# A hybrid recurrent layer: causal scores written by masked copies of VectorE and by ScalarE, gate product on VectorE

## The chip, the cores and the metric

The kernel runs on one core of a Trainium2 chip. A core has five engines that run side by side, each with its own list of instructions: PE (TensorE, matrix products, with PEld loading its weights), DVE (VectorE), ACT (ScalarE), POOL (GpSimd) and SP (SyncE, which here starts the DMA transfers). They meet only at semaphores. PE writes its results into PSUM, which DVE and ACT read; all other tiles lie in SBUF. The metric is the device time of one execution in microseconds (us): the median of three executions before the change is 2206.64 us (2205.87 to 2207.19).

## The reference, cut to what matters

One decoder layer on 2048 tokens of width 1024: an RMS norm, one input projection whose columns feed two token mixers, an output projection with residual, a SwiGLU feed-forward, a last norm. The change touches both mixers. The first (HGRN2, 4 heads of width 128) works on groups of 32 tokens:

```python
causal = jnp.tril(jnp.ones((CHUNK, CHUNK), dtype=bool))          # CHUNK = 32
def step(state, xs):
    q_, k_, lg, v_ = xs
    b = jnp.cumsum(lg, axis=-2)
    q_dec, k_dec = q_ * jnp.exp(b), k_ * jnp.exp(-b)
    scores = jnp.where(causal, jnp.einsum('bhtk,bhsk->bhts', q_dec, k_dec), 0.0)
    o = jnp.einsum('bhts,bhsv->bhtv', scores, v_) + jnp.einsum('bhtk,bhkv->bhtv', q_dec, state)
    ...
```

The second (RG-LRU, width 512 in 4 units of 128) computes `b_in = sqrt(-expm1(2 log_a)) * (ig * xc)` and a linear recurrence over the tokens. The product `ig * xc` is the other part that the change touches.

## The kernel before

The tokens are worked in two halves of 1024; each half has two chunks c of 512 tokens, and a chunk is four tiles of 128. A half runs a projection pv (the values), eight steps s, a gate projection pg, the output projection with residual, and the feed-forward. Full float precision is got by splitting each operand into a high and a low part, so a projection of one chunk is 24 matmuls of 128x512 (three per block of 128 inputs, L225 to L227).

A step projects two times 128 features, for chunk 0 and then chunk 1, into the PSUM banks pa and pb. Even steps (0, 2, 4, 6) are the four HGRN heads: `hg_pre` (sigmoids, logarithm, the scan L250 and some twenty small products) runs on ACT and DVE, and `hg_mid` and `hg_post` are put off into the projections of the step behind it. Odd steps are the four RG-LRU units (`lru_pre`, `lru_post`). Names carry their place: pb_3_0 is pb of step 3, chunk 0; sct_77 and sct_79 are the two score tiles that chunks 0 and 1 use in turn.

In `hg_mid` PE transposes the decayed keys into the bank pk (L320), DVE copies them to kut (L322), PE computes the scores of a chunk into the bank pc by 16 small matmuls (L329). The kernel works on tiles of 128 tokens, not of 32, and a score tile is stored transposed: rows are the source tokens, columns the target tokens, and only columns from a row's own block of 32 on are written by PE. Four DVE copies (L341) take these into the tile sct, each 32 columns of all four token tiles. Then POOL's affine_select (L342) sets to zero what lies below the diagonal. PE makes the state updates pu (L347), and DVE adds them up (L352, S and the carry). In `hg_post` PE computes the output po from the states (L364) and from the scores (L365), in turn for four tiles; ACT squares it (L370), POOL takes the inverse root, DVE scales it into v (L373). In `lru_post` POOL does the product ig * xc (L414); DVE and ACT do the rest.

The order on every engine isn't written out: the program is traced in the order of the code, and a scheduler with its own estimate of durations then puts each engine's instructions in order and adds the semaphores. Instructions of two engines that use the same PSUM bank are kept in order among each other. So an edit to a few lines can move instructions all over the input-projection stage.

Of the kernel before, what the change touches and what calls it, by code (L numbers as in the profile page):

```python
# [8 lines left out]
F32 = mybir.dt.float32  # L9
F32R = mybir.dt.float32r  # L10
AF = mybir.ActivationFunctionType
ALU = mybir.AluOpType

P = 128
# [9 lines left out]
CW = 512  # L24
NC = T // CW
TPC = CW // P
NTT = T // P
SUB = 32
# [7 lines left out]
def hybrid_layer(ctx: ExitStack, tc: tile.TileContext, x, x_t, norm_w, cols, w_in, gate_w, w_out, w_gu, w_down, out):  # L36
    nc = tc.nc
    const = ctx.enter_context(tc.tile_pool(name="const", bufs=1))
    sb = ctx.enter_context(tc.tile_pool(name="sb", bufs=1))
# [23 lines left out]
    def late(nm):  # L63
        return sb.tile([P, CW], F32, tag="late", name=nm, bufs=5)
# [4 lines left out]
    def aux(nm):  # L69
        return psp.tile([P, CW], F32, tag="aux", name=nm)  # L70
# [4 lines left out]
    mask = const.tile([P, CW], mybir.dt.bfloat16, name="mask")  # L75
    nc.gpsimd.memset(mask, 1.0)
    nc.gpsimd.memset(mask.rearrange("p (n s) -> p n s", s=SUB)[:, :, 0:1], 0.0)
    sc_t = []
    for i in range(2):
        s = const.tile([P, TPC, P], F32, name=f"sct{i}")  # L80
# [8 lines left out]
    v = nc.vector  # L89
# [225 lines left out]
    def hg_mid(h, c, st, vt, nm):  # L315
        hs = slice(h * P, (h + 1) * P)
        W, Wy, K, KU, G = (st[k] for k in ("W", "Wy", "K", "KU", "G"))
        pk = aux("pk" + nm)
        for n in range(TPC):
            nc.tensor.transpose(out=pk[:, n * P : (n + 1) * P], in_=KU[:, n * P : (n + 1) * P], identity=ident)  # L320
        kut = late("kut" + nm)
        v.tensor_copy(out=kut, in_=pk)  # L322

        pc = aux("pc" + nm)
        for n in range(TPC):
            o = n * P
            for j in range(4):
                r0 = j * SUB
                nc.tensor.matmul(  # L329
                    pc[r0 : r0 + SUB, o + r0 : o + P],  # L330
                    lhsT=K[:, o + r0 : o + r0 + SUB],
                    rhs=(W if j < 2 else Wy)[:, o + r0 : o + P],
                    start=True,
                    stop=True,
                )
        sc = sc_t[flip[0] % 2]
        flip[0] += 1
        pc4 = pc.rearrange("p (n t) -> p n t", t=P)
        for j in range(4):
            rows, cs = slice(0, (j + 1) * SUB), slice(j * SUB, (j + 1) * SUB)  # L340
            v.tensor_copy(out=sc[rows, :, cs], in_=pc4[rows, :, cs])  # L341
        nc.gpsimd.affine_select(  # L342
            out=sc, in_=sc, pattern=[[0, TPC], [1, P]], compare_op=ALU.is_ge, fill=0.0, base=0, channel_multiplier=-1
        )
        pu = aux("pu" + nm)
        for n in range(TPC):
            nc.tensor.matmul(pu[:, n * P : (n + 1) * P], lhsT=kut[:, n * P : (n + 1) * P], rhs=vt[:, n, hs], start=True, stop=True)  # L347

        S = late("S" + nm)
        states = [carry[:, c % 2, h, :]] + [S[:, n * P : (n + 1) * P] for n in range(TPC - 1)] + [carry[:, 1 - c % 2, h, :]]  # L350
        for n in range(TPC):
            v.scalar_tensor_tensor(  # L352
                out=states[n + 1], in0=states[n], scalar=G[:, n, 3:4], in1=pu[:, n * P : (n + 1) * P], op0=ALU.mult, op1=ALU.add
            )
        st["S"], st["sc"] = states, sc
# [44 lines left out]
    def lru_post(u, gl, xc, xh, xl, y, nm):  # L400
        pr, pi = aux("pr" + nm), aux("pi" + nm)
        for m, pg in enumerate((pr, pi)):
            gs = slice((m * NU + u) * P, (m * NU + u + 1) * P)
            nc.tensor.matmul(pg, lhsT=gwh[:, gs], rhs=xh, start=True, stop=False)
            nc.tensor.matmul(pg, lhsT=gwl[:, gs], rhs=xh, start=False, stop=False)
            nc.tensor.matmul(pg, lhsT=gwh[:, gs], rhs=xl, start=False, stop=True)
        r, ig, t = late("r" + nm), late("ig" + nm), late("t" + nm)
        us = slice(u, u + 1)
        nc.scalar.activation(out=r, in_=pr, func=AF.Sigmoid, bias=par[:, C_BA + u : C_BA + u + 1])
        nc.scalar.activation(out=ig, in_=pi, func=AF.Sigmoid, bias=par[:, C_BX + u : C_BX + u + 1])  # L410

        nc.scalar.activation(out=t, in_=r, func=AF.Tanh, scale=msp[:, us])
        nc.scalar.activation(out=r, in_=r, func=AF.Exp, scale=nmsp[:, us])
        nc.gpsimd.tensor_tensor(out=ig, in0=ig, in1=xc, op=ALU.mult)  # L414
        v.tensor_tensor(out=xc, in0=r, in1=r, op=ALU.mult)
        v.scalar_tensor_tensor(out=t, in0=xc, scalar=1.0, in1=t, op0=ALU.add, op1=ALU.mult)
        nc.scalar.activation(out=t, in_=t, func=AF.Sqrt)
        v.tensor_tensor(out=ig, in0=ig, in1=t, op=ALU.mult)
        v.tensor_tensor_scan(out=t, data0=r, data1=ig, initial=hst[:, us], op0=ALU.mult, op1=ALU.add)
        nc.gpsimd.tensor_copy(out=hst[:, us], in_=t[:, CW - 1 : CW])  # L420
        v.tensor_tensor(out=y[:, u, :], in0=t, in1=gl, op=ALU.mult)
# [454 lines left out]
    for half in range(2):  # L876
# [36 lines left out]
        for s in range(8):  # L913
            i = s // 2
            ws.ahead(2)
            wa, wb = ws.take(2)
            ws.ahead(2)
            for c in range(NC):
                nm = f"{half}_{s}_{c}"
                pa = feat_mm(wa, xt[c], "pa" + nm)  # L920
                run_pending()
                pb = feat_mm(wb, xt[c], "pb" + nm)
                if s % 2 == 0:
                    st = hg_pre(i, pa, pb, nm)
                    nxt = [
                        lambda i=i, st=st, c=c, nm=nm: hg_mid(i, c, st, vts[c], nm),
                        lambda i=i, st=st, c=c, nm=nm: hg_post(i, st, vts[c], nm),
                    ]
                else:
                    r = lru_pre(i, pa, pb, nm)  # L930
                    nxt = [lambda i=i, r=r, c=c, nm=nm: lru_post(i, *r, ys[c], nm)]
                pend.append(nxt)
# [175 lines left out]
```

## Time and profile before

| | before |
|---|---|
| median of three executions | 2206.64 us |
| the profiled execution, its span | 2208.05 us, 2206.3 us |
| mean granted clock of TensorE | 0.985 of full speed |
| busy: PE | 2121.9 us, 96% |
| busy: DVE, ACT, POOL | 1508.5, 1019.4, 587.7 us |

The span runs from the first to the last instruction of the profiled execution. PE is busy nearly throughout; the view of waits names what it waited for, and for how long, and the timeline lists instructions with their start, duration and, in brackets, the idle time of their engine before them with what ended it. The granted clock is the share of full speed (2.4 GHz) at which PE was allowed to run. The steps of the first half lie between about 75 and 360 us, those of the second between about 500 and 800 us.

### The profile page before, as it was taken

The numbers are of one execution on the slowest core, as the hardware profiler recorded it, in microseconds if no ns is written. First come the engines' busy times: TensorE is split into PE (matmuls) and PEld (weight loads), VectorE is DVE, ScalarE is ACT, GpSimd is POOL, SyncE is SP. The second block draws the span as 40 slices with busy tenths as digits, with TensorE's granted clock in tenths as the row PEclk, the third lists the DMA queues.
The fourth block names the chain that finished last, engine by engine and source line by source line (L and its number), as shares of the span: only waits on it lengthen the run. The fifth ranks groups of instructions, "written<-read, shape, count | busy, mean of one in ns | idle before, by whom it ended". The sixth has DMA issues, their size and how long they took to land. (4 is left out here: it accounts for less than half of the span.)

```text
span 2206.3 us, 27183 instructions
## 1 busy us (share of the span) xinstructions
PE 2121.9 (96%) x9956; PEld 1744.7 (79%) x9956; DVE 1508.5 (68%) x2314; ACT 1019.4 (46%) x1757; POOL 587.7 (27%) x442
## 2 busy tenths in 40 slices
PE   8999899999999999999999998998999999998998
PEld 6778788887777887788888876887788888876876
DVE  5566664635677557866676579777767666679897
ACT  5467664535677545433333343444333333343443
POOL 1111110101111101223232146411323232356455
PEclk9999999999999999999999999999999999999999
DMA  6111105851110056423232264355423232355423
GB/s 220 58 39 39 39 20 169 285 167 30 38 39 29 20 181 230 150 98 106 91 125 91 96 227 164 115 160 169 134 91 124 91 124 91 105 209 196 153 86 139
DMA packets 137414, 261.33 MB, mean 118 GB/s; under 512 B 11072, under 2 KB 27456, under 8 KB 137280
## 3 DMA queue, kind: packets, MB, share of 16 engines
q1 hardware_dynamic: 137280, 259.59, 35.1%
q8 instruction: 78, 1.28, 0.2%
q14 instruction: 56, 0.46, 0.1%
HBM read 196.37 MB, written 63.18 MB: 118 GB/s over the span
## 5 line engine op out<-in xcount | busy, mean ns | idle before, releaser
L484 POOL TENSOR_TENSOR e<-u,e 128x512 f32<-128x512 f32 x44 | 77.3, 1757 | 525.3 <-ACT wgu_c L198 307.0
L484 POOL TENSOR_TENSOR hd<-hd,e 128x512 f32<-128x512 f32 x80 | 121.5, 1550 | 142.4 <-DVE e L484 142.3
L582 PE MATMUL quad_e<-act_e,wgu_e 128*128 128x512 f32 x528 | 129.2, 393 | 2.0 <-ACT wgu_e L198 1.9
L582 PE MATMUL quad_f<-act_f,wgu_f 128*128 128x512 f32 x528 | 127.1, 389 | 1.5 <-ACT wgu_f L198 1.5
L582 PE MATMUL quad_g<-act_d,wgu_d 128*128 128x512 f32 x528 | 127.6, 390 | 0.0
L582 PE MATMUL quad_a<-act_a,wgu_a 128*128 128x512 f32 x528 | 127.3, 389 | 0.0
L582 PE MATMUL quad_g<-act_g,wgu_g 128*128 128x512 f32 x528 | 127.1, 389 | 0.0
L582 PE MATMUL quad_a<-act_b,wgu_b 128*128 128x512 f32 x528 | 127.0, 389 | 0.0
L582 PE MATMUL quad_e<-act_c,wgu_c 128*128 128x512 f32 x528 | 126.8, 389 | 0.0
L582 PEld LDWEIGHTS quad_e<-act_e,wgu_e 128*128 128x128 f32 x528 | 100.1, 190 | 24.0 <-ACT wgu_e L198 2.6
L582 PEld LDWEIGHTS quad_f<-act_f,wgu_f 128*128 128x128 f32 x528 | 99.1, 188 | 22.4 <-ACT wgu_f L198 1.8
L582 PEld LDWEIGHTS quad_a<-act_a,wgu_a 128*128 128x128 f32 x528 | 98.9, 188 | 20.9 <-issue 0.4
L582 PEld LDWEIGHTS quad_a<-act_b,wgu_b 128*128 128x128 f32 x528 | 99.1, 188 | 20.6
L582 PEld LDWEIGHTS quad_e<-act_c,wgu_c 128*128 128x128 f32 x528 | 99.1, 188 | 20.6
L582 PEld LDWEIGHTS quad_g<-act_g,wgu_g 128*128 128x128 f32 x528 | 99.0, 188 | 20.6
L582 PEld LDWEIGHTS quad_g<-act_d,wgu_d 128*128 128x128 f32 x528 | 98.9, 188 | 20.4
L484 DVE TENSOR_TENSOR u<-u,quad_g 128x512 f32<-128x512 f32 x88 | 60.4, 686 | 79.3 <-PE quad_g L582 79.2
L226 PE MATMUL pb<-xn,wlo_in 128*128 128x512 f32 x256 | 102.7, 401 | 0.0
L225 PE MATMUL pb<-xn,whi_in 128*128 128x512 f32 x256 | 102.4, 400 | 0.0
L227 PE MATMUL pb<-xn,whi_in 128*128 128x512 f32 x256 | 101.8, 398 | 0.0
L155 DVE TENSOR_TENSOR wlo_in<-raw_in,whi_in 128x1024 fp32r<-128x1024 f32 x48 | 60.7, 1265 | 60.0 <-PE pv L238 40.6
L226 PE MATMUL pa<-xn,wlo_in 128*128 128x512 f32 x256 | 100.9, 394 | 0.0
(316 smaller groups left out, 5521.2 us busy)
## 6 DMA issues: line engine op xcount, KB each, us to landing
raw<-in_w_gu SPq DMA_DIRECT2D x88, 512.0 KB, 3.8
raw_in<-in_w_in SPq DMA_DIRECT2D x48, 512.0 KB, 3.5
ao_p<-as SPq DMA_DIRECT2D x76, 256.0 KB, 2.3
raw_o<-in_w_out SPq DMA_DIRECT2D x32, 512.0 KB, 4.7
x<-in_x SPq DMA_DIRECT2D x32, 256.0 KB, 5.3
xrh<-in_x SPq DMA_DIRECT2D x32, 256.0 KB, 3.9
h<-h SPq DMA_DIRECT2D x32, 256.0 KB, 3.7
hn<-hths SPq DMA_DIRECT2D x32, 256.0 KB, 4.5
```

Source lines behind the costliest of these rows:

```text
L155: v.tensor_tensor(out=lo, in0=raw, in1=f(hi), op=ALU.subtract)
L225: nc.tensor.matmul(ps, lhsT=whi[:, ks], rhs=hi, start=(k == 0), stop=False)
L226: nc.tensor.matmul(ps, lhsT=wlo[:, ks], rhs=hi, start=False, stop=False)
L227: nc.tensor.matmul(ps, lhsT=whi[:, ks], rhs=lo, start=False, stop=(k == KT - 1))
L484: (e or v).tensor_tensor(out=out, in0=a, in1=b, op=op)
L582: nc.tensor.matmul(ps, lhsT=w[:, s, ks], rhs=x, start=first and k + n == 0, stop=k == 3 and n == 2, skip_group_check=not first)
```

## The change

A constant `keep` is built once: a causal 32x32 mask of bytes, repeated in each of the four groups of 32 partitions. The four copies and the affine_select are replaced: for each group j of 32 rows, DVE copies the 32x32 diagonal block of each of the four token tiles from pc to sct where the mask is set (copy_predicated), and ACT copies the columns to the right of it (96, 64 and 32 columns per tile; none for j = 3). What lies below the diagonal is not written any more; sct is set to zero at the start, as before. In `lru_post` the product ig * xc moves from POOL to DVE.

```diff
--- before.py
+++ after.py
@@ -75,6 +75,15 @@
     mask = const.tile([P, CW], mybir.dt.bfloat16, name="mask")
     nc.gpsimd.memset(mask, 1.0)
     nc.gpsimd.memset(mask.rearrange("p (n s) -> p n s", s=SUB)[:, :, 0:1], 0.0)
+
+    keep = const.tile([P, SUB], mybir.dt.uint8, name="keep")
+    tri = sb.tile([P, CW], F32, tag="pg", name="tri", bufs=16)
+    nc.gpsimd.memset(tri, 1.0)
+    nc.gpsimd.affine_select(
+        out=tri[:, 0:P], in_=tri[:, 0:P], pattern=[[1, P]], compare_op=ALU.is_ge, fill=0.0, base=0, channel_multiplier=-1
+    )
+    for j in range(4):
+        nc.gpsimd.tensor_copy(out=keep[j * SUB : (j + 1) * SUB], in_=tri[j * SUB : (j + 1) * SUB, j * SUB : (j + 1) * SUB])
     sc_t = []
     for i in range(2):
         s = const.tile([P, TPC, P], F32, name=f"sct{i}")
@@ -337,11 +346,10 @@
         flip[0] += 1
         pc4 = pc.rearrange("p (n t) -> p n t", t=P)
         for j in range(4):
-            rows, cs = slice(0, (j + 1) * SUB), slice(j * SUB, (j + 1) * SUB)
-            v.tensor_copy(out=sc[rows, :, cs], in_=pc4[rows, :, cs])
-        nc.gpsimd.affine_select(
-            out=sc, in_=sc, pattern=[[0, TPC], [1, P]], compare_op=ALU.is_ge, fill=0.0, base=0, channel_multiplier=-1
-        )
+            rows, cs = slice(j * SUB, (j + 1) * SUB), slice(j * SUB, (j + 1) * SUB)
+            v.copy_predicated(out=sc[rows, :, cs], mask=keep[rows].unsqueeze(1).broadcast_to([SUB, TPC, SUB]), data=pc4[rows, :, cs])
+            if j < 3:
+                nc.scalar.copy(out=sc[rows, :, (j + 1) * SUB : P], in_=pc4[rows, :, (j + 1) * SUB : P])
         pu = aux("pu" + nm)
         for n in range(TPC):
             nc.tensor.matmul(pu[:, n * P : (n + 1) * P], lhsT=kut[:, n * P : (n + 1) * P], rhs=vt[:, n, hs], start=True, stop=True)
@@ -411,7 +419,7 @@
 
         nc.scalar.activation(out=t, in_=r, func=AF.Tanh, scale=msp[:, us])
         nc.scalar.activation(out=r, in_=r, func=AF.Exp, scale=nmsp[:, us])
-        nc.gpsimd.tensor_tensor(out=ig, in0=ig, in1=xc, op=ALU.mult)
+        v.tensor_tensor(out=ig, in0=ig, in1=xc, op=ALU.mult)
         v.tensor_tensor(out=xc, in0=r, in1=r, op=ALU.mult)
         v.scalar_tensor_tensor(out=t, in0=xc, scalar=1.0, in1=t, op0=ALU.add, op1=ALU.mult)
         nc.scalar.activation(out=t, in_=t, func=AF.Sqrt)
```

Behind the inserted lines the code's line numbers are 9 higher up to the scores and 8 higher behind them (L320 becomes L329, L365 becomes L373).

The change moves instructions only in the steps of the two halves and at the start. Three places show how. First PE behind the pending head of step 2 (first half, inside the projections of step 3), before:

```order
L226 MATMUL pb_3_0_1468<-xn_0_01_155,wlo_in_11_1129 128x512
L347 MATMUL pu_2_0_1299<-v_0_381,kut_2_0_1275 128x128 x4
L364 MATMUL po_2_0_1411<-carry,QI_2_0_1229 128x128
L227 MATMUL pb_3_0_1468<-xn_0_11_157,whi_in_11_1128 128x512
L225 MATMUL pb_3_0_1468<-xn_0_01_155,whi_in_11_1128 128x512
L365 MATMUL po_2_0_1411<-v_0_381,sct_77 128x128
L226 MATMUL pb_3_0_1468<-xn_0_01_155,wlo_in_11_1129 128x512
L320 MATMUL pk_2_1_1429<-ident,lg_2_1_1336 128x128 x4
```

And after (rows left out are more of pb_3_0 and pa_3_1):

```order
L235 MATMUL pb_3_0_1484<-xn_0_00_162,wlo_in_11_1141 128x512
L355 MATMUL pu_2_0_1313<-v_0_389,kut_2_0_1287 128x128 x4
L372 MATMUL po_2_0_1425<-carry,QI_2_0_1241 128x128
L236 MATMUL pb_3_0_1484<-xn_0_10_164,whi_in_11_1140 128x512
...
L236 MATMUL pb_3_0_1484<-xn_0_11_165,whi_in_11_1140 128x512
L329 MATMUL pk_2_1_1443<-ident,lg_2_1_1350 128x128 x4
L234 MATMUL pa_3_1_1524<-xn_1_00_494,whi_in_10_1134 128x512
...
L373 MATMUL po_2_0_1425<-v_0_389,sct_85 128x128
L372 MATMUL po_2_0_1425<-S_2_0_1318,QI_2_0_1241 128x128
L373 MATMUL po_2_0_1425<-v_0_389,sct_85 128x128
```

The first product with the states (po) still follows pu, but the first product with the scores (sct) has moved from two rows behind it to behind the rest of pb_3_0, the transposes pk_2_1 of chunk 1 and four rows of pa_3_1.

Then DVE in the same place, before (eB, G, QI, W, nx and lg are small products of `hg_pre` for chunk 1, S and carry the state updates of chunk 0):

```order
L322 COPY kut_2_0_1275<-pk_2_0_1270 128x512
...
L305 TENSOR_TENSOR lg_2_1_1336<-sf_2_1_1335,lg_2_1_1336 128x8x32
L341 COPY sct_77<-pc_2_0_1277 32x4x32
L341 COPY sct_77<-pc_2_0_1277 64x4x32
L341 COPY sct_77<-pc_2_0_1277 96x4x32
L341 COPY sct_77<-pc_2_0_1277 128x4x32
...
L306 TENSOR_TENSOR lg_2_1_1336<-nx_2_1_1345,G_2_1_1353 128x8x32
...
L352 SCALAR_TENSOR_TENSOR S_2_0_1304<-carry,G_2_0_1224,pu_2_0_1299 128x128
L352 SCALAR_TENSOR_TENSOR S_2_0_1304<-S_2_0_1304,G_2_0_1224,pu_2_0_1299 128x128 x2
L352 SCALAR_TENSOR_TENSOR carry<-S_2_0_1304,G_2_0_1224,pu_2_0_1299 128x128
```

And after:

```order
L285 COPY eB_2_1_1365<-eb_2_1_1358 128x16
L331 COPY kut_2_0_1287<-pk_2_0_1282 128x512
...
L303 TENSOR_TENSOR eb_2_1_1358<-sq_2_1_1348,nx_2_1_1359 128x4x32
L350 COPY_PREDICATED sct_85<-keep,pc_2_0_1289 32x4x32
L314 TENSOR_TENSOR lg_2_1_1350<-sf_2_1_1349,lg_2_1_1350 128x8x32
...
L350 COPY_PREDICATED sct_85<-keep,pc_2_0_1289 32x4x32
L315 TENSOR_TENSOR lg_2_1_1350<-nx_2_1_1359,G_2_1_1367 128x8x32
L310 TENSOR_TENSOR QI_2_1_1372<-W_2_1_1373,eB_2_1_1365 128x4x64
L350 COPY_PREDICATED sct_85<-keep,pc_2_0_1289 32x4x32
L360 SCALAR_TENSOR_TENSOR S_2_0_1318<-carry,G_2_0_1236,pu_2_0_1313 128x128
L360 SCALAR_TENSOR_TENSOR S_2_0_1318<-S_2_0_1318,G_2_0_1236,pu_2_0_1313 128x128
L350 COPY_PREDICATED sct_85<-keep,pc_2_0_1289 32x4x32
```

The four copies that stood together are now four masked copies spread between the products of the next chunk, the last of them between the state updates (the other two updates follow it), and kut stands directly behind eB.

Last ACT in the same place, before (lg is the last exponential of `hg_pre` of chunk 1, xp the copy that feeds the next RG-LRU unit, ojk the squares):

```order
L271 ACTIVATE lg_2_1_1336<-lg_2_1_1336 128x512
L381 COPY xp_3_0_1493<-pa_3_0_1386 128x512
L370 ACTIVATE ojk_2_0_1421,oss_2_0_1420<-po_2_0_1411 128x128 x4
L384 ACT_TABLE_LOAD
L384 ACTIVATE gl_3_0_1497<-pb_3_0_1468 128x512
```

And after:

```order
L280 ACTIVATE lg_2_1_1350<-lg_2_1_1350 128x512
L389 COPY xp_3_0_1509<-pa_3_0_1400 128x512
L352 COPY sct_85<-pc_2_0_1289 32x4x96
L352 COPY sct_85<-pc_2_0_1289 32x4x64
L352 COPY sct_85<-pc_2_0_1289 32x4x32
L392 ACT_TABLE_LOAD
L392 ACTIVATE gl_3_0_1513<-pb_3_0_1484 128x512
```

The three new copies stand behind xp and ahead of the squares, and the gelu (gl) has moved ahead of the squares.

## Rows read from the trace of the kernel before

**Rows 1.** The page's first part: busy us, share of the span, instructions.

```profile
PE 2121.9 (96%) x9956; PEld 1744.7 (79%) x9956; DVE 1508.5 (68%) x2314; ACT 1019.4 (46%) x1757; POOL 587.7 (27%) x442
```

**Rows 2.** PE's waits, whole run: us in total, times, longest.

```profile
PE po L365 <- POOL sct L342: 13.4, 6, 2.8
PE pk L320 <- DVE lg L306: 8.1, 2, 4.1
PE pu L347 <- DVE kut L322: 2.0, 4, 0.9
```

**Rows 3.** PE's timeline, first half: start us, us, instruction [idle before <-releaser].

```profile
97.27 0.80 PE L365 MATMUL po<-v,sct 128*128 128x128 f32 x2 [2.83 <-POOL sct L342]
...
116.96 0.48 PE L225 MATMUL pb<-xn,whi_in 128*128 128x512 f32 x1
...
148.81 0.60 PE L320 MATMUL pk<-ident,lg 128*128 128x128 f32 x4
...
150.33 0.50 PE L227 MATMUL pa<-xn,whi_in 128*128 128x512 f32 x1
...
156.24 1.16 PE L347 MATMUL pu<-v,kut 128*128 128x128 f32 x8 [0.85 <-DVE kut L322]
...
160.43 0.49 PE L365 MATMUL po<-v,sct 128*128 128x128 f32 x2 [2.34 <-POOL sct L342]
...
222.59 0.49 PE L365 MATMUL po<-v,sct 128*128 128x128 f32 x2 [1.53 <-POOL sct L342]
...
273.18 0.63 PE L320 MATMUL pk<-ident,lg 128*128 128x128 f32 x4 [4.07 <-DVE lg L306]
```

**Rows 4.** Windows: length, busy of PE, PEld, DVE, ACT, POOL; clock, DMA share, GB/s.

```profile
94.40:97.20 2.80, 0.04 (x1) 0.00 (x0) 2.77 (x12) 0.01 (x1) 2.80 (x2) 0.95 0.00 0
96.90:100.30 3.40, 3.03 (x8) 2.55 (x9) 2.72 (x6) 0.00 (x0) 0.45 (x2) 0.50 0.00 0
...
161.80:165.10 3.30, 3.30 (x25) 2.84 (x16) 0.52 (x1) 0.00 (x0) 0.00 (x0) 0.50 0.00 0
...
222.60:226.00 3.40, 3.40 (x46) 2.60 (x47) 3.25 (x7) 0.62 (x1) 0.00 (x0) 1.00 0.02 5
...
274.40:277.80 3.40, 3.40 (x18) 2.42 (x10) 3.37 (x15) 2.76 (x6) 0.14 (x1) 0.50 0.26 96
```

**Rows 5.** The chain that ended last, one piece of the last stage.

```profile
2039.02 21.76 PE pdb L834 x96
```

**Rows 6.** Instructions by line: duration ns min/median/max, first and last start us.

```profile
L342 POOL TENSOR_SCALAR_AFFINE_SELECT sct<-sct x16: 634/1150/4819, 92.4 to 712.6; 128x512 f32<-128x512 f32 x16
...
L341 DVE COPY sct<-pc x64: 268/269/278, 91.5 to 712.2; 32x128 f32<-32x128 f32 x16, 64x128 f32<-64x128 f32 x16, 96x128 f32<-96x128 f32 x16, 128x128 f32<-128x128 f32 x16
...
L370 ACT ACTIVATE ojk<-po x64: 268/278/288, 104.8 to 729.3; 128x128 f32<-128x128 f32 x64
...
L381 ACT COPY xp<-pa x16: 567/579/591, 92.5 to 718.0; 128x512 f32<-128x512 f32 x16
...
L416 DVE SCALAR_TENSOR_TENSOR t<-xc,t x16: 681/684/692, 124.8 to 747.0; 128x512 f32<-128x512 f32 x16
```

**Rows 7.** DVE's timeline: the start, step 0, step 2.

```profile
8.61 1.42 DVE L434 SCALAR_TENSOR_TENSOR x<-x,ss_x,wmix 128x512 f32<-128x512 f32 x2 [3.50 <-DMA wmix<-in_norm_w]
...
95.71 0.33 DVE L352 SCALAR_TENSOR_TENSOR S<-carry,G,pu 128x128 f32<-128x128 f32 x1
...
140.14 0.18 DVE L276 COPY eB<-eb 128x16 f32<-128x16 f32 x1 [2.73 <-ACT eb L253]
...
147.78 0.42 DVE L306 TENSOR_TENSOR lg<-nx,G 128x256 f32<-128x256 f32 x1
...
154.19 0.17 DVE L276 COPY eB<-eb 128x16 f32<-128x16 f32 x1
```

**Rows 8.** ACT's timeline, step 2.

```profile
153.52 0.63 ACT L253 ACTIVATE eb<-b 128x512 f32<-128x512 f32 x1 [0.44 <-DVE b L250]
...
165.53 0.28 ACT L370 ACTIVATE ojk<-po 128x128 f32<-128x128 f32 x1 [9.62 <-PE po L365]
```

## The prediction, made before the change was run

> **What bounds the kernel now.** I read the page's busy times first: TensorE (PE) is busy 96% of the span [rows 1], so time can go only where PE stands still or runs slowly. The view of PE's waits says where it stands still beside the edited code: 13.4 us, in six waits, at the score product L365 for the POOL mask L342; 8.1 us in two waits at the transposes L320 (pk) for DVE's L306; 2.0 us in four at L347 (pu) for DVE's copy L322 [rows 2]. PE's timeline gives their order in the first half: 2.83 at 97.27 (step 0), 0.85 and 2.34 before 156.24 and 160.43 (step 2), 1.53 at 222.59 (step 4), 4.07 at 273.18 (step 6) [rows 3]. These five make 11.6 us, and half of the three totals (23.5) is 11.8: the second half of the tokens repeats the first.
>
> Waits cost twice where the clock follows them. In the 3.4 us after the 2.83, after the 0.85 with the 2.34, and after the 4.07, the granted clock is 0.50, the lower of the two levels; after the lone 1.53 it is 1.00 [rows 4]. Half of 3.4 us is lost each time, 1.7 us, three times in a half: 5.1 us. At full clock a row of 128x512 takes 21.76/96 = 0.227 us [rows 5].
>
> The mask itself has a median of 1.15 us, a minimum of 0.63 and a maximum of 4.82, the one that starts at 92.4 [rows 6]. It ends just before PE's 2.83 us wait; in that wait POOL is busy for all of 2.80 us with it and DVE for 2.77, with 12 instructions [rows 4]. POOL is slow while DVE is dense.
>
> **The change, part by part.** *Mask removed.* L342 leaves the path from pc to L365. Four copies L341 and 0.63 to 4.82 us become seven pieces that alternate DVE, ACT, DVE, ... because all read one PSUM bank. None of the seven is in the trace. A masked copy writes 32 partitions x 128: its nearest row, L341's, takes 0.27 [rows 6], and I take that; the upper bound is 0.42, a 256-element product [rows 7], the lower 0.20, a guess at what is left where it overlaps its neighbours. ACT's pieces of 384, 256 and 128 elements lie between a 128-element square from PSUM, 0.28, and a 512-element copy from PSUM, 0.58 [rows 6]; on that line 0.48, 0.38 and 0.28, together 1.14. So an undisturbed chain is 4 x 0.27 + 1.14 + six handovers of about 0.04 (ACT's eb ends at 153.52 + 0.63, DVE's eB starts at 154.19 [rows 7, 8]) = 2.5 us.
>
> It isn't undisturbed: its four DVE links stand between products. I replay DVE's new list of step 2 with the old durations: eB at 154.19 [rows 7], then kut, which now stands directly behind it, ends at 154.96; the first masked copy starts at about 156.6, the second at 158.6 (behind eight products), the third at 159.4, the fourth at 160.3 behind two state updates of 0.33 [rows 7]. The scores are whole at about 160.65. ACT's links fit in between: ACT idles for 9.62 us before its squares at 165.53 [rows 8]. That idle time hides the 1.14 us per unit that ACT gains.
>
> *PE's order moves with it.* The built program puts the rest of the score products (L365 before, L373 now) behind nearly the whole pb of the next unit and behind pk of the second chunk, where before two pb rows lay between. In step 0 there are 20 pb rows, one pa row and pk in place of those two. PE came to L365 at 97.27 - 2.83 = 94.44; 19 rows of 0.227 and four transposes (0.60 [rows 3]) later it is 99.3. The last masked copy stands ahead of the first state update, which started at 95.71 [rows 7]; pushed back by ACT's links it ends at about 96.6. Wait 0, margin 2.7.
>
> Step 2: the first pb row behind the last L365 of the head before started at 116.96 [rows 3]. From there it is 142 full rows to pk, 1.5 us for pk and pc (148.81 to 150.33 [rows 3]), and 14 rows to pu: 156 x 0.227 + 1.5 = 36.9, so PE comes at 153.9, and kut is ready at 155.0. A wait of about 1.2 stays at pu. Then pu and the first L364 (1.2), 16 pb rows, pk and four pa rows (5.1): 161.3 at the score product, the scores at 160.65. Margin 0.6, wait 0.
>
> Steps 4 and 6: ACT's new list between a head's last squares and the next exponentials is the one that step 2 had, so I time them by step 2's rows. Step 4 has 140 rows to pk and 21 to pu; kut stands six instructions later on DVE, so again 1.2 at pu, and 1.2 at pk of the second chunk, which follows two pb rows behind pu and waits for L315 (L306 before). Step 6 has 132 rows to pk, so PE is there at 147.0 by step 2's count. L306 ended at 148.20 [rows 7]; it now stands ahead of a 512- and a 256-element product, some 0.9 earlier: of the 4.07 about 0.3 is left. Then 14 rows to pu, reached after 34.7, where kut, behind the scan, comes after 37.3: 2.6. The score product waits 0 to 0.4.
>
> Waits of a half after: 1.2 + 2.4 + 2.9 = 6.5, against 11.8. Gain 5.3 per half, 10.6 in all.
>
> *Clock.* In steps 0 and 2 no wait of more than 1.2 is left, and the lone 1.53 brought no fall [rows 4]. The 2.6 of step 6 is nearly the 2.83 that did. I count one fall per half in place of three, with 0 to 2 possible: 3.4 us per half, 6.8 in all.
>
> *Product L414 from POOL to DVE (L422).* A product of this shape takes DVE 0.68 (L416 [rows 6]); 16 of them are 11 us. They lie in the odd steps, where DVE still idles, as for 2.73 us before 140.14 [rows 7]. Hidden, I take 0. With the cover gone, steps 2, 4 and 6 begin 0.68 later: 3 x 0.68 x 2 = 4.1 us. A gain below nothing: POOL's slowness beside DVE goes both ways if they share something, so DVE may get back a few tenths per unit; I leave that out.
>
> *Mask constant.* Six POOL instructions at the start; DVE's first product stands there until 8.61, 3.50 us of it for a weight vector from DMA [rows 7]. Nothing. In the feed-forward and output stages the order is unchanged: 0.
>
> **A rule against the change.** The four L341 copies all start at partition 0. Three of the four masked copies start at partitions 32, 64 and 96, and no row of before shows such a neighbourhood. The Trainium skill, "VectorE: DVE Perf Modes", section "Two Vector instructions with no wait between them", says that an instruction whose operand starts in another group of 32 partitions than its predecessor's is held until all earlier ones have ended. By it each of these copies and its follower would lose their overlap, an estimated 0.07 each, some 0.45 us per unit: step 2's margin of 0.6 nearly goes, step 6 waits 0.4 more, and the gain would be about 1 us smaller.
>
> **The sum.** 10.6 + 6.8 = 17.4 us. The profiled execution took 2208.05 (span 2206.3 and 1.75 around it), so 2190.65; it lies 1.41 above the median of 2206.64, so 2189.2 on the median's basis. Its own range: no falls 2185.8; two falls per half 2192.6; masked copies at 0.42 add 0.6 per unit, about 1.5 per half, 3 in all. With the replayed waits uncertain by 1 us per half: 2184 to 2197.
>
> **The rivals.** *ACT bounds steps 2, 4 and 6.* The added copies and two more table loads lie in the queue that feeds the exponentials; then the waits there only change names, and step 0 alone gains: 2 x (2.83 + 1.7) = 9.1, so 2197.6. For it: pk and kut hang on ACT's eb (DVE idles for it before 140.14 [rows 7]). Against: the copies stand behind that work, in 9.62 us of idle time.
>
> *The product is not covered:* 17.4 - 4.1 = 13.3, so 2193.3.
>
> *The waits only move:* what PE no longer waits for at L365 it waits for at pu and pk, and the clock falls as before: 2206.6, give or take 3. For it: kut and pk depend on DVE and ACT, not on POOL, and the new order keeps 1 to 3 us of wait there.
>
> *The alternation is slow* (slower than before). Seven links pass between two queues. If each costs x more than the rows say, the scores come 7x later. The margins of steps 0, 2, 4 and 6 are about 2.7, 0.6, 0.4 and 0, so the waits at the score product are 28x - 3.7 per half, and each of four brings the clock down, with the one counted five falls, 8.5 us. A half then has 6.5 + 28x - 3.7 + 8.5, against 11.8 + 5.1 = 16.9 before. It breaks even at x = 0.20 us and is 0.2% slower from 0.28; at 0.30 it is 2.8 worse per half: 2212.2. For it: no row shows a masked copy, and DVE's queue is dense there. Against: the bounds from the rows leave at most 0.15 per masked copy.
>
> **How the numbers follow.** Forecast 0.53; ACT bounds 0.14; product uncovered 0.07; waits only move 0.10; slow alternation 0.16. A measurement of this kernel tells 0.2%, 4.4 us, from no change. The first three are faster, 0.74; same 0.10; slower 0.16. The range, 2183 to 2207, reaches over the first three and half of the fourth.
>
> **What would show it.** Right: no wait at the score product in steps 0 and 2; waits of 1 to 3 us at pu; a clock of 1.00 in the stretches behind 97 and 161 us; masked copies of about 0.27; ACT's three copies ahead of the squares. Wrong: a wait of over 1 us at the score product, masked copies over 0.45, pk waiting in all three steps, or as many half-clock stretches as before.

## The result, and the profile after

The changed kernel has a median of 2188.82 us (2187.45 to 2189.57, four runs), the kernel before, on the same chip, 2206.26: a ratio of 0.992, with a 95% interval of 0.9903 to 0.9937. The prediction was 2189.2, with a range of 2183 to 2207. The profiled executions are further apart than the medians: spans of 2185.7 and 2206.3 us, 20.6 us. Of one experiment, E10, the profiled execution ran at a granted clock of 0.847 (2360.16 us) and is left out, so its waits are not shown.

The first part of the page after [rows 1 has PE's line of before]:

```profile
PE 2114.0 (97%) x9956; PEld 1739.3 (80%) x9956; DVE 1516.5 (69%) x2330; ACT 1038.1 (47%) x1807; POOL 551.3 (25%) x416
```

PE is busy for 8 us less with the same 9956 matmuls, mostly since 13.6 us less of the run was at half clock, which is worth 6.8; POOL lost 36 us of work, DVE and ACT gained 8 and 19.

PE's waits after, in the first half (60 to 360 us; us in total, times, longest):

```profile
PE pu L355 <- DVE kut L331: 3.8, 3, 1.9
PE pk L329 <- DVE lg L315: 1.3, 2, 1.0
```

The score product is gone from this list [rows 2]; what is left is 5.1 us in a half. In the second half pu has 3.9 and pk 1.3. PE's timeline after, at the places of [rows 3]:

```profile
99.61 0.27 PE L329 MATMUL pk<-ident,lg 128*128 128x128 f32 x1
99.72 0.39 PE L373 MATMUL po<-v,sct 128*128 128x128 f32 x2
...
112.54 0.47 PE L236 MATMUL pb<-xn,whi_in 128*128 128x512 f32 x1
...
152.42 0.82 PE L355 MATMUL pu<-v,kut 128*128 128x128 f32 x5 [1.95 <-DVE kut L331]
...
158.44 0.40 PE L234 MATMUL pa<-xn,whi_in 128*128 128x512 f32 x1
158.67 0.42 PE L373 MATMUL po<-v,sct 128*128 128x128 f32 x2
...
210.84 1.16 PE L355 MATMUL pu<-v,kut 128*128 128x128 f32 x8 [0.87 <-DVE kut L331]
...
213.69 0.63 PE L329 MATMUL pk<-ident,lg 128*128 128x128 f32 x4 [1.00 <-DVE lg L315]
...
266.32 1.16 PE L355 MATMUL pu<-v,kut 128*128 128x128 f32 x8 [1.00 <-DVE kut L331]
```

In step 0 PE goes from the transposes straight into the score product (L373, 99.72), and in step 2 from the fourth row of pa (158.44) at 158.67: no wait. The waits that stayed are at pu, 1.95, 0.87 and 1.00, and at the transposes, 0.31 in step 2 and 1.00 in step 4. The clock in stretches behind such waits (columns as in [rows 4]):

```profile
154.00:157.40 3.40, 3.40 (x17) 2.73 (x16) 3.31 (x14) 0.83 (x2) 2.05 (x1) 1.00 0.00 0
268.00:271.40 3.40, 3.40 (x16) 2.82 (x15) 3.31 (x17) 1.24 (x4) 0.58 (x1) 1.00 0.01 2
568.00:571.40 3.40, 3.40 (x13) 2.82 (x12) 3.34 (x16) 0.81 (x3) 2.06 (x1) 0.50 0.01 2
827.40:830.80 3.40, 3.40 (x10) 2.62 (x9) 3.40 (x6) 1.09 (x2) 0.00 (x0) 0.51 0.91 285
```

Behind 1.95 us the clock stays at 1.00, and behind the 1.00 of step 6 too. In the second half the same wait, 1.99 us before 567.20, was followed by 3.4 us at 0.50. The fourth row lies in the output projection, which the change doesn't touch: a fall that the profiled execution of before doesn't have there.

DVE's and ACT's timelines after, in step 2:

```profile
151.68 0.69 DVE L331 COPY kut<-pk 128x512 f32<-128x512 f32 x1
...
153.97 0.28 DVE L350 COPY_PREDICATED sct<-keep,pc 32x128 f32<-32x128 uint8 x1
154.16 0.41 DVE L314 TENSOR_TENSOR lg<-sf,lg 128x256 f32<-128x256 f32 x1
...
155.59 0.41 DVE L309 TENSOR_TENSOR W<-QI,eB 128x256 f32<-128x256 f32 x1
156.03 0.29 DVE L350 COPY_PREDICATED sct<-keep,pc 32x128 f32<-32x128 uint8 x1
156.35 0.43 DVE L315 TENSOR_TENSOR lg<-nx,G 128x256 f32<-128x256 f32 x1
...
158.24 0.30 DVE L350 COPY_PREDICATED sct<-keep,pc 32x128 f32<-32x128 uint8 x1
```

```profile
152.74 0.57 ACT L389 COPY xp<-pa 128x512 f32<-128x512 f32 x1
154.28 0.47 ACT L352 COPY sct<-pc 32x384 f32<-32x384 f32 x1 [0.98 <-DVE sct L350]
156.35 0.36 ACT L352 COPY sct<-pc 32x256 f32<-32x256 f32 x1 [1.60 <-DVE sct L350]
157.49 0.26 ACT L352 COPY sct<-pc 32x128 f32<-32x128 f32 x1 [0.77 <-DVE sct L350]
...
160.47 0.28 ACT L378 ACTIVATE ojk<-po 128x128 f32<-128x128 f32 x1 [0.82 <-PE po L373]
```

Each of ACT's copies starts 0.03 to 0.04 us after the end of the masked copy that it waits for. DVE's next masked copy comes 0.4 to 1.3 us behind ACT's end, since it stands behind other products in DVE's list. ACT's three copies stand in time that was idle. And the durations of the new instructions (ns min/median/max):

```profile
L350 DVE COPY_PREDICATED sct<-keep,pc x64: 278/296/311, 92.4 to 696.6; 32x128 f32<-32x128 uint8 x64
...
L352 ACT COPY sct<-pc x48: 256/363/471, 92.9 to 696.3; 32x384 f32<-32x384 f32 x16, 32x256 f32<-32x256 f32 x16, 32x128 f32<-32x128 f32 x16
...
L422 DVE TENSOR_TENSOR ig<-ig,xc x16: 691/693/694, 116.6 to 721.7; 128x512 f32<-128x512 f32 x16
```

### The profile page after: what moved, and what is told of

The parts are those of the page before. It is cut to its first block, busy times and chain, and to the rows that moved or that the text cites. A ratio compares the mean times of both kernels' runs of the same rounds, so it can differ in the third digit from the quotient of the medians.

```text
span 2185.7 us, 27177 instructions
## 1 busy us (share of the span) xinstructions
PE 2114.0 (97%) x9956; PEld 1739.3 (80%) x9956; DVE 1516.5 (69%) x2330; ACT 1038.1 (47%) x1807; POOL 551.3 (25%) x416
## 5 line engine op out<-in xcount | busy, mean ns | idle before, releaser
L590 PEld LDWEIGHTS quad_a<-act_b,wgu_b 128*128 128x128 f32 x528 | 99.1, 188 | 20.6
L590 PEld LDWEIGHTS quad_e<-act_c,wgu_c 128*128 128x128 f32 x528 | 99.1, 188 | 20.6
L590 PEld LDWEIGHTS quad_g<-act_g,wgu_g 128*128 128x128 f32 x528 | 99.0, 188 | 20.6
L590 PEld LDWEIGHTS quad_a<-act_a,wgu_a 128*128 128x128 f32 x528 | 99.0, 188 | 20.5
L247 PE MATMUL poh<-wlo_o,mx 128*128 128x512 f32 x256 | 100.2, 394 | 0.6 <-DVE wlo_o L164 0.6
```

The lines of the kernel that those rows point to most:

```text
L247: nc.tensor.matmul(ps, lhsT=hi, rhs=wlo[:, ks], start=False, stop=False)
L590: nc.tensor.matmul(ps, lhsT=w[:, s, ks], rhs=x, start=first and k + n == 0, stop=k == 3 and n == 2, skip_group_check=not first)
```

## The experiments

All are timed against the kernel before on the same chip; its medians there are 2205.25 to 2206.34 us. "Steps" is the time from the start of the last matmul of pv to the start of the first of the output projection, in the first and the second half, on PE's timeline of the profiled execution; "waits" is PE's idle time in it; "half" is the time in it at a granted clock of 0.50.

| kernel | median us | ratio, interval | steps us | waits us | half us |
|---|---|---|---|---|---|
| before | 2206.26 | | 286.3, 286.3 | 12.1, 11.9 | 10.2, 10.2 |
| changed | 2188.82 | 0.9903 to 0.9937 | 274.5, 276.0 | 5.1, 5.2 | 0, 3.4 |
| E1 masked only | 2191.20 | 0.9921 to 0.9946 | 277.8, 276.2 | 6.4, 6.4 | 3.4, 0 |
| E2 product only | 2206.85 | 0.9996 to 1.0014 | 285.2, 283.7 | 11.9, 11.8 | 6.8, 3.4 |
| E3 four from zero | 2195.01 | 0.9932 to 0.9957 | 280.1, 277.8 | 7.2, 7.4 | 6.8, 0 |
| E4 mask kept | 2197.93 | 0.9954 to 0.9979 | 279.8, 279.8 | 8.2, 8.2 | 3.4, 3.4 |
| E5 kut on ACT | 2190.89 | 0.9925 to 0.9950 | 278.6, 277.3 | 7.7, 7.8 | 3.4, 0 |
| E6 masked twice | 2205.54 | 0.9988 to 1.0006 | 284.4, 285.1 | 11.4, 12.0 | 10.2, 10.2 |
| E8 four, kut on ACT | 2190.39 | 0.9920 to 0.9942 | 277.5, 277.5 | 5.0, 5.0 | 6.8, 6.8 |
| E11 kut first | 2181.78 | 0.9879 to 0.9906 | 271.9, 272.0 | 1.7, 1.7 | 0, 0 |
| E12 four, kut first | 2184.23 | 0.9887 to 0.9919 | 273.7, 273.5 | 4.3, 4.2 | 0, 0 |
| E13 before, kut first | 2228.96 | 1.0078 to 1.0107 | 298.8, 296.5 | 20.6, 20.5 | 23.9, 20.5 |

One line fits the rows: 269.6 us per half, a constant fitted to them, plus the waits, plus half of the time at half clock. Before: 269.6 + 12.1 + 5.1 = 286.8 for 286.3; changed: 274.7 for 274.5 and 276.5 for 276.0; E11: 271.3 for 271.9. All are within 0.8 us but E6 (1.6 to 1.8) and E13 (3.4 to 3.8). In E13 low-clock stretches overlap PE's own idle time by 3.8 and 5.2 us, so 1.9 and 2.6 us are counted twice; in E6 the overlap is 0.4 and 1.8 us and explains 0.2 and 0.9. What is left there, 0.7 to 1.6 us, is open. The line is bookkeeping: it says that PE's work at full clock is the same in all these orders, and that a kernel's time in the steps differs by its waits and its time at half clock. What causes a wait is read from the experiments below.

**E1, masked only.** The edit takes one line back:

```diff
-        v.tensor_tensor(out=ig, in0=ig, in1=xc, op=ALU.mult)
+        nc.gpsimd.tensor_tensor(out=ig, in0=ig, in1=xc, op=ALU.mult)
```

> One part alone: scores by masked copies and ScalarE as in the changed kernel, but the product ig*xc stays on POOL. Theory (the mask's removal and the order that follows it give the gain, the product nothing): 2189 us, 2185 to 2193, no wait of over 0.5 us at the score product. Rival (the product is part of the gain): 2195 to 2203.

2191.2: the masks give nearly all of the gain. The expectation of no wait over 0.5 us was missed in step 6, where 0.6 us came back at the score product and 1.3 at the state product behind it. Moving the product as well is worth 2.4 us by the medians; the intervals overlap, so this isn't shown to differ from nothing.

**E2, product only.** The kernel before with that line on VectorE.

> The other part alone: only the product ig*xc moves to VectorE, the four copies and POOL's mask stay. Theory: 2206 us, 2203 to 2209, with the same 6 to 7 us per half of wait at the score product for POOL's mask and the 4 us at the transposes of step 6. Rival (POOL without the product finishes its masks sooner, or VectorE without POOL beside it is faster): 2195 to 2201.

2206.85, no change. The waits of [rows 2] are there nearly as before:

```profile
PE po L365 <- POOL sct L342: 6.0, 3, 2.8
PE pk L320 <- DVE lg L306: 4.8, 3, 3.3
PE pu L347 <- DVE kut L322: 0.9, 1, 0.9
```

**E3, four from zero.** VectorE alone, four masked copies at the places of the old ones:

```diff
-            rows, cs = slice(j * SUB, (j + 1) * SUB), slice(j * SUB, (j + 1) * SUB)
-            v.copy_predicated(out=sc[rows, :, cs], mask=keep[rows]..., data=pc4[rows, :, cs])
-            if j < 3:
-                nc.scalar.copy(...)
+            rows, cs = slice(0, (j + 1) * SUB), slice(j * SUB, (j + 1) * SUB)
+            v.copy_predicated(out=sc[rows, :, cs], mask=keep[rows, cs]..., data=pc4[rows, :, cs])
```

> No mask on POOL and no ScalarE: VectorE copies the same four pieces as the kernel before, all from partition 0, but with a mask of 128x128 bytes; product on VectorE. TensorE's order is then nearly that of before: the score product follows the first state product directly. Theory (the mask itself was the wait): the 6.7 us per half at the score product shrink to under 1, two of three clock falls per half go, the 4 us at the transposes of step 6 stay: 2187, 2183 to 2192; the masked copies start 0.20 to 0.22 apart as the plain ones did. Rival (the moved order hides the wait, not the shorter chain): 1 to 2 us per step stay at the score product, 2196 to 2203. Rival (a masked copy is held like those that start in another quadrant): starts 0.30 or more apart.

2195.0, between the two ranges. Its waits, and its masked copies on DVE's timeline:

```profile
PE pk L328 <- DVE lg L314: 4.2, 3, 3.3
PE po L371 <- DVE sct L350: 1.0, 2, 0.7
PE po L370 <- DVE S L358: 0.9, 1, 0.9
PE pu L353 <- DVE kut L330: 0.8, 1, 0.8
```

```profile
153.51 0.87 DVE L350 COPY_PREDICATED sct<-keep,pc 32x128 f32<-32x128 uint8 x4
```

The score product's wait fell from 6.7 to 1.0 us per half, as the first theory said; but 0.9 came up at the state product (L370), the transposes of step 6 kept their 3.3, and with them the clock fell for 6.8 us in the first half. In the steps it gains 14.7 us of the change's 22.1 (572.6 less 557.9 and 550.5). The rest of the change's gain is in these other waits and their clock falls, which hang on the order that the scheduler made. The alternation isn't needed for it: E12 below has four copies and gains more than the change. The four copies take 0.87 together, 0.20 apart, as the plain ones: the third expectation fell.

**E4, mask kept.** The changed kernel with POOL's affine_select behind the pieces.

> The changed kernel with POOL's mask put back behind the seven pieces (it changes no value). TensorE's order stays close to that of the changed kernel: the score product stands 16 to 20 rows later than before. Theory (the mask's time is the wait): waits of 1 to 3 us return at the score product in steps 0, 2, 4 and 6 with their clock falls, 2196 to 2206. Rival (the moved order alone hides it): none over 0.5 us, 2187 to 2192.

2197.9, in the first theory's range, but not for its reason. The waits and the mask:

```profile
PE pu L358 <- DVE kut L331: 7.2, 3, 2.6
...
PE po L376 <- POOL sct L353: 0.5, 2, 0.3
```

```profile
L353 POOL TENSOR_SCALAR_AFFINE_SELECT sct<-sct x16: 634/635/1617, 97.7 to 706.3; 128x512 f32<-128x512 f32 x16
```

Only 0.5 us per half is at the score product: the moved order hides the mask, as the rival said, and the mask itself is short there (median 0.635). The time went to pu, 2.6 us in steps 4 and 6 each. In step 4 this program has 18 rows ahead of the transposes and 15 ahead of pu, in place of 20 and 21: eight rows, 1.8 us, which is the difference to the 0.87 of the changed kernel. In step 6 kut stands behind one more product of VectorE; the rest of that wait I did not separate.

**E5, kut on ScalarE**, and **E8**, the same with four masked copies from partition 0 on VectorE:

```diff
-        v.tensor_copy(out=kut, in_=pk)
+        nc.scalar.copy(out=kut, in_=pk)
```

> The changed kernel with the copy kut (pk from PSUM) on ScalarE instead of VectorE. Theory A (the wait left at pu comes from the exponential eb that both queues follow: ScalarE too gets to kut only behind eb and one nx, at about the 152.3 us of before): waits of 1.5 to 2.5 us stay at pu in steps 2, 4 and 6, and 2188.8 becomes 2190 to 2195. Theory B (VectorE's queue alone makes kut late): the 3.8 us per half at pu go, 2179 to 2184.

> Four masked copies from partition 0 on VectorE, and kut on ScalarE. The order moves again: 17 to 18 rows between the scores and pu, 4 to 8 rows between pu and the score product. Theory A (time = 269.6 us per half in the steps + TensorE's waits + 1.7 us per clock fall): waits of 0.5 to 1.5 us at pu, under 0.7 at the score product, the 3.3 us at the transposes of step 6 gone, since 20 rows stand there in place of 27: 4 to 6 us of wait per half and at most one fall: 2186 to 2192. Theory B (the alternation with ScalarE is what brings the gain): 2195 or more, as with the four copies alone.

E5 is 2190.9, by theory A. On ACT's timeline in step 2 kut stands behind eb and one nx, and ends at 152.72, where VectorE's ended at 152.37:

```profile
151.32 0.63 ACT L262 ACTIVATE eb<-b 128x512 f32<-128x512 f32 x1 [0.45 <-DVE b L259]
151.85 0.40 ACT L279 ACTIVATE nx<-b 128x256 f32<-128x256 f32 x1
152.16 0.56 ACT L331 COPY kut<-pk 128x512 f32<-128x512 f32 x1
```

PE waits 1.9 to 2.0 at pu in each step. E8 is 2190.4, in theory A's range, and has 5.0 us of wait per half, all at pu; but two of the waits, 2.05 and 2.40, are longer than its 1.5, and there are two clock falls per half where at most one was expected.

**E6, masked twice.** The line with copy_predicated stands twice in the changed kernel.

> The changed kernel with each masked copy done twice (no value changes): 4 x 0.3 us more VectorE work per unit inside the alternating chain. Theory A (the length of the chain counts only as far as TensorE's order doesn't cover it; this program puts 20 to 24 rows of projection, 5 us, between pu and the score product): no wait of over 0.7 us at the score product, 2186 to 2194. Theory B (links on the chain cost time whatever the order): 1.2 to 2.4 us of wait per unit at the score product in steps 0 to 6, with clock falls, 2200 to 2212.

2205.5: the time is theory B's, the place is neither's. Nothing over 0.4 us stands at the score product; it came up at the transposes:

```profile
PE pk L329 <- DVE lg L315: 10.3, 3, 4.3
```

They wait for L315, a product of VectorE's that comes late in this order: in step 2 it ends at 151.10, in the changed kernel at 145.27. Each chain got four times 0.3 us longer; besides, the masked copies stood idle for ACT's pieces for 11.0 us in the whole run, against 3.2 in the changed kernel, and PE's and DVE's orders moved. So the time added to VectorE is paid at a later deadline and not at the score product; how much of it each of the three causes has I did not separate.

**E10, pu written later**, behind the scores with the output products, in the four-copy kernel:

> Four masked copies from partition 0 on VectorE, and the state updates pu are written in the code behind the scores, together with the output products, so that the order repeats itself in steps 2, 4 and 6: 18 rows, transposes, scores, 15 rows, pu, 4 rows, score product. Theory A (time = 269.6 us per half in the steps + waits + 1.7 us per fall): with 15 rows instead of 21 TensorE reaches pu early, so 2 to 2.7 us of wait at pu in each of the three steps, 6 to 8 per half, and one or two falls: 2192 to 2198. Theory B (a regular order is better whatever its rows): 2185 to 2190.

2198.3 (0.9951 to 0.9977), just above theory A's range. That the time goes to pu, as the theory says, is not shown.

**E11, kut first**, on the changed kernel; **E12**, on the four-copy kernel; **E13**, on the kernel before. One line makes the next chunk's scan, which reads the mask, wait for kut:

```diff
         v.tensor_copy(out=kut, in_=pk)
+        v.tensor_scalar(out=mask[:, 0:1], in0=kut[:, 0:1], scalar1=0.0, scalar2=None, op0=ALU.mult)
```

> The changed kernel with one tiny VectorE instruction behind kut that writes zero into the first column of the scan's mask (which is zero anyway): so the scan of the next chunk, and with it eb, must come behind kut. Theory A (the waits left at pu come only from kut standing behind that scan and eb): kut ends near 150.3 instead of 152.4 in step 2, the 3.8 us per half at pu shrink to under 1, no wait over 0.5 at the score product with 24 rows and more before it, and without waits of 2 us no clock falls: 2177 to 2184. Theory B (the scan and all behind it come 0.8 later, which costs what kut gains): 2186 to 2192, the wait moving to the transposes or the score product.

> The same dependency with four masked copies from partition 0 on VectorE and nothing on ScalarE. Theory A: as the other one, 2177 to 2184, with the score product one row behind the first state product and the four copies directly behind the scan, so no wait over 0.7 there. Theory B (the alternation with ScalarE is needed, because it makes the order put rows before the score product): waits of 1 to 2 us at the score product in steps 2, 4 and 6, 2188 to 2196.

E11 is 2181.8, the best of all: 7.0 us below the changed kernel by the medians and 6.2 by the ratios, with intervals that barely overlap, and every wait at pu is gone. DVE's timeline in step 2, and what is left of PE's waits:

```profile
149.02 0.55 DVE L258 TENSOR_SCALAR sf<-sf,tinies 128x512 f32<-128x512 f32 x1 [0.69 <-ACT lg L257]
149.48 0.68 DVE L331 COPY kut<-pk 128x512 f32<-128x512 f32 x1
150.20 0.16 DVE L332 TENSOR_SCALAR mask<-kut 128x1 bf16<-128x1 f32 x1
150.39 1.23 DVE L259 TENSOR_TENSOR_SCAN b<-mask,lg 128x512 f32<-128x512 bf16 x1
```

```profile
PE pk L329 <- DVE lg L315: 1.7, 2, 1.1
```

Kut ends at 150.16 in place of 152.37, before the scan and eb instead of behind them. E12, 2184.2, is at the edge of theory A and below theory B's range. Three waits of 0.6 at the score product and one of 1.8 at pu are left, and one of 0.6 at pk:

```profile
PE po L372 <- DVE sct L351: 1.8, 3, 0.6
PE pu L354 <- DVE kut L330: 1.8, 1, 1.8
PE pk L328 <- DVE lg L314: 0.6, 1, 0.6
```

> The kernel before, with POOL's mask and POOL's product, and only the dependency of the scan's mask on kut added. It tells whether that dependency needs the change. Theory A (POOL's mask under a dense VectorE is a wait of its own): 3 to 6 us of wait per half stay at the score product, 2196 to 2204. Theory B (kut's place is all, the mask is hidden once kut comes early): under 1 us at the score product, 2180 to 2188.

E13 went the other way: 2229.0, 0.92% slower, and no theory had that. Waits, and a window over one of POOL's masks:

```profile
PE po L366 <- POOL sct L343: 12.9, 3, 5.6
PE pk L320 <- DVE lg L306: 6.2, 3, 4.1
```

```profile
157.90:163.60 5.70, 0.13 (x1) 0.00 (x0) 5.66 (x25) 2.89 (x5) 5.68 (x2) 0.83 0.00 0
```

The dependency puts the long run of small products of `hg_pre` beside POOL's mask: DVE is busy for 5.66 of 5.70 us, and the mask takes all of it. The median mask takes 2.39 us in this kernel, the longest 7.47 [rows 6 has 1.15 and 4.82]. So the line that gives 6 to 7 us behind the change costs 22.6 ahead of it.

DVE's being busy isn't enough to slow the mask. In the kernel before one mask runs beside the copy kut, which reads PSUM and takes all of DVE's time:

```profile
227.27 0.64 POOL L342 TENSOR_SCALAR_AFFINE_SELECT sct<-sct 128x512 f32<-128x512 f32 x1 [4.74 <-DVE sct L341]
227.32 0.67 DVE L322 COPY kut<-pk 128x512 f32<-128x512 f32 x1
```

The masks of over 3 us, here and in the kernel before, run beside products most of which read two tiles in SBUF. That this is the difference fits the rows, but no run varied it alone.

## Why the prediction was right, step by step

- **The mask off the path.** Shown. Waits at the score product went from 6.7 us per half to none. E2 shows that the product's move doesn't do it, E3 that the shorter chain does it nearly alone (1.0 left), E4 that the moved order can hide a mask of 0.6 us as well. "POOL is slow while DVE is dense" was too wide: the text on E13 has a mask of 0.64 beside a DVE without a gap. Predicted waits of 6.5 per half were 5.1 and 5.2; the gain in waits is 13.7 (24.0 less 10.3), not 10.6.
- **The sizes of that step.** Step 2's pu: 1.2 predicted, 1.95 measured, since, counted from the first pb row (112.54), PE came after 37.9 (36.9 replayed) and kut after 39.9 (38.0). Step 4: 1.2 and 1.2, measured 0.87 and 1.00. Step 6: 2.6 at pu and 0.3 at pk predicted, 1.00 and nothing measured: the largest error of a term, and it made the forecast too cautious; 0.3 at pk came in step 2. Both replays took the scan that goes ahead of kut to start 35.3 after the first pb row, as in step 2 of before; it started after 37.1 in step 2 and after 34.2 in step 6. What moved it is open.
- **The clock.** One fall per half was counted; the profiled execution has none in the first and one in the second, behind 1.99 us. 5 falls went, worth 8.5 us (17.0 us at half clock), 6.8 predicted. Which of two nearly equal waits, 1.95 and 1.99, is followed by a fall these rows don't tell, so a count of falls is partly luck.
- **New pieces.** Masked copies 0.296 (0.27 taken), ACT's 0.26, 0.36 and 0.47 (0.28, 0.38, 0.48), handovers to ACT 0.03 (0.04). The slow alternation would have needed 0.28 us more per link; a masked copy takes 0.03 more, ACT's pieces less. This rival is out by the trace.
- **The rule on partitions.** The trace agrees with the Trainium skill's "VectorE: DVE Perf Modes", "Two Vector instructions with no wait between them". The first masked copy, at partition 0, overlaps its neighbours: 154.16 follows 153.97. The second, at partition 32, starts at 156.03, 0.03 after L309 ended (155.59 + 0.41), and its follower at 156.35, 0.03 after its end. From start to start these are 0.44 and 0.32, where DVE has 0.34 behind another product of that size (154.16 to 154.50) and 0.20 behind the first masked copy: about 0.10 lost on either side, an estimated 0.6 per unit, where 0.45 was predicted. Step 2's margin was put at 0.6 without this loss and is 0.13: the scores are whole at 158.54 (158.24 + 0.30), and PE comes at 158.67. In E3, with all at partition 0, nothing is lost.
- **The product.** Taken as hidden, and E1 agrees: with it on POOL the kernel is not faster. The rival of an uncovered product is out. The gain that was left out, VectorE's instructions freed of POOL, is real but small: the copy xp of three columns took up to 0.60 us in the kernel before and takes 0.17 at most now.
- **The other rivals.** ACT as the bound is out: its copies stand in idle time, no wait of PE's ends at ACT, and the waits at pu go when kut's place alone moves (E11). "The waits only move" is true of a small part: pu went from 1.0 to 3.8 us per half, while the waits as a whole went from 12.1 to 5.1.
- **Why the sum met the median.** Partly by chance. In the steps the profiled pair differs by 22.1 us, more than the 17.4 predicted: the terms erred by 3.1 in the waits and 1.7 in the clock, 4.8 us. Against that, 1.7 went to a fall in the output projection, and the profiled pair lies further apart than the medians, on whose basis the number was put: the execution of before is 1.8 above its median (2208.05, 2206.26), that of after 1.4 below (2187.45, 2188.82). These make 4.9, and the two cancel. Executions of one kernel differ in their falls: of the 50 of the kernel before that were timed with the experiments, those at a mean clock of 0.984 have a median of 2208.5 us, those at 0.988 one of 2203.3. Where these falls lie isn't on record, as only one execution was profiled.

## What to carry to other kernels

Price a stage by two sums from the trace, the waits of the engine that is full and its time at the lower clock, and read each edit by which wait it moves; here that line held in ten kernels of twelve (E6 and E13 are off). With a scheduler that orders the engines, an edit's largest effect may be another instruction's place: look in the new order at what stands between a copy and the one who needs it, and, where a copy is late only by its place, a dependency puts it right. Try such a dependency on the final kernel: the same line gave 6 to 7 us here and cost 22.6 there.

## What the runs showed of the hardware

- A POOL pass over a 128x512 tile takes 0.63 to 0.64 us with VectorE idle (E4, at 646.3), and 0.64 also beside a VectorE copy from PSUM without a gap (before, at 227.27); beside VectorE's products, most of them of two tiles in SBUF, it took up to 7.47 (E13, at 223.39).
- VectorE is slowed as well: a product of 256 elements took 0.70 us beside a mask (E4, at 97.89), where the others of that size take 0.41.
- VectorE's masked copies overlap their neighbours at partition 0 (0.20 apart, 0.28 each, E3) and not at partitions 32 to 96 (0.03 from end to start, changed kernel).
- Whether a wait of PE is followed by half clock isn't settled by its length in these runs. The two halves of one kernel differ: E2's 2.82 in step 0 was followed by a fall in the first half, not in the second, E3's 3.3 in step 6 likewise; 1.95 was not and 1.99 was in the changed kernel; of six waits of 1.91 to 1.96 in E5 one was. In the steps of these kernels the shortest wait followed by a fall is 1.27 (E1, 1.3 us behind one of 0.59), and no shorter one was.
